# Small weight parts last in every split product, block 1 and the context in one pass, modulation steps in the middle MLP groups

## The chip, the core and the metric

The kernel runs on one core of one Trainium2 chip. The metric is the device time of one execution in microseconds (us). Three executions of the kernel before took 3923.38, 3931.42 and 3940.43 us, so the median is 3931.42 us. The profiled execution is another one, of 3930.93 us.

## What is computed

The reference is a backbone of two layers on 1024 latent tokens and 256 context tokens of width 1024. Each layer makes modulation vectors (six shift, scale and gate vectors of width 1024, for the latent tokens and for the context), a token mixer and an MLP with squared ReLU:

```python
for l in range(DEPTH):                                    # DEPTH = 2
    sh1, sc1, gt1, sh2, sc2, gt2 = adaln(c, w_ada[l], b_ada[l])        # silu(c) @ w + b, six parts
    csh1, ...                    = adaln(c_ctx, w_ada[l], b_ada[l])
    h_lat = rms_norm(x, g_attn_pre[l]) * (1 + sc1) + sh1               # h_ctx alike
    y_lat, y_ctx = hybrid_mixer(h_lat, h_ctx, ...)        # w_in; gated DeltaNet, RG-LRU, attention; w_out
    x = x + gt1 * rms_norm(y_lat, g_attn_post[l])
    h = rms_norm(x, g_mlp_pre[l]) * (1 + sc2) + sh2
    x = x + gt2 * rms_norm(square(relu(h @ w_mlp1[l])) @ w_mlp2[l], g_mlp_post[l])
    if l == 0:                                            # the context takes the same steps
        ctx = ...
```

In the last layer the context feeds the mixer, but its own output is not computed.

## The kernel before, in words

Activations are kept transposed, 128 channels on the partitions and tokens along the free axis. Tokens are cut in three blocks: "c" (256 context tokens), 0 and 1 (512 latent tokens each). The large products (w_in, w_out, both MLP matrices) are made with split operands: a weight tile `wr` of 128x1024 is loaded, ScalarE copies it to `wh` in a shorter format (the large part), and GpSimd subtracts to get `wl`, the small part (`weight`, L209; for the context alone VectorE makes every second `wl`). The activations are split in the same way: a tile `A` or `hid` holds both parts. `mm3` (L223) makes one output tile of 128 rows as 24 matmuls (12 in the second MLP matrix): for each of eight slices k of the contraction it multiplies large by large, large weight by small activation, small weight by large activation. Only the last of the three reads `wl`. The tags `wr`, `wh` and `wl` have two buffers each, so a weight's load starts when the split of the weight but one before it is done.

`layer` (L1151) first runs the mixer, then w_out (8 weights), then the MLP in eight groups of four weights up (w_mlp1) and four down (w_mlp2). w_out and the first two and last two MLP groups run as passes, one block at a time, each with its own loads of the weights; the four groups in the middle take all blocks with one load. The passes let the work between two products (`around`: the root mean square of the output, scale, residual, the next norm; two sums of squares by a product with `ones`, L186, and two broadcasts by transposes, L192) run behind the next pass. These four small products stand at fixed places in TensorE's stream, given as "behind the n-th output tile from here" (`put_behind`), and TensorE works in order, so it waits where they are not ready. In layer 0 the passes are 0, 1, "c"; in layer 1 they are 0, 1.

The modulation vectors are made by a list of background steps, `bg`. `tick(n)` (L321) takes up to n steps off the list. `weight` calls `tick(self.rate)`, `mla_attend` calls `tick(1)` for each chunk of keys, and `run` calls `tick(99)` once at the start. There are two kinds of step:

- `ada_pe` (L263): one step loads 128x1024 of w_ada and multiplies it on TensorE (two matmuls of 32x512). Layer 0's vectors 0 and 1 are made so at the start (16 loads, with eight buffers of their own); its vectors 2, 3 and 4 by 26 further steps (24 loads, 2 closing steps) that take the buffers of `wr`, one for each chunk of keys in the attention of layer 0.
- `ada_steps` (L294): one step loads 512x256 of w_ada into a `wr` buffer and accumulates it on VectorE in eight instructions; every second step closes with four one-column matmuls (L314). Vector 5 of a layer and vectors 0 to 4 of the next are made so: 48 steps in layer 0, 8 in layer 1. Before, the list is set after pass 0; one step goes with each weight of pass 1 (16 weights), the rest with the 32 weights of the middle groups.

All engines' orders are set when the program is built, by a scheduler that goes by priorities and its own estimates; on the chip each engine takes its instructions in that order, and SyncE's queue issues the loads and stores in its order.

Of the kernel before, what the change touches and what calls it, by code (L numbers as in the profile page):

```python
# [7 lines left out]
F32 = mybir.dt.float32  # L8
# [8 lines left out]
P = 128  # L17
D = 1024
KD = D // P
# [24 lines left out]
class Trunk:  # L44
    def __init__(self, tc, I, out, es):
        self.tc, self.nc, self.I, self.out = tc, tc.nc, I, out
        nc = self.nc
        self.cp = es.enter_context(tc.tile_pool(name="cp", bufs=1))
        self.open = {}
        self.wp = es.enter_context(tc.tile_pool(name="wp", bufs=1))  # L50
        self.tp = es.enter_context(tc.tile_pool(name="tp", bufs=1))
        self.dp = es.enter_context(tc.tile_pool(name="dp", bufs=1, space=DRAM))
        self.ps = es.enter_context(tc.tile_pool(name="ps", bufs=1, space=PSUM))
        self.n = self.ng = self.flip = self.ht = 0
        self.bg, self.rate, self.wpr = [], 0, 0
        self.held = []
        self.main = self.cur = ("s", (self.tp, 4), ["a", "st", "d"])
        self.cst = self.cp.tile([P, 5 * P], F32, name="cst")
        nc.sync.dma_start(self.cst, I["cst"])
        self.ident = self.cst[:, 0:128]  # L60
        self.mask = [self.cst[:, 128:256], self.cst[:, 256:384]]
        self.tri = [self.cst[:, 384:512], self.cst[:, 512:640]]
        self.ones = self.cp.tile([P, 128], F32, name="ones")
        nc.vector.memset(self.ones, 1.0)
        self.sil = self.cp.tile([P, KD, 32], F32, name="sil")
# [156 lines left out]

    def mm3(self, ps, w, acts, ks):  # L223

        nc = self.nc
        n, last = 0, 3 * len(ks) - 1
        for wk, a in zip(ks, acts):
            for wi, ai in ((0, 0), (0, 1), (1, 0)):
                mm = nc.tensor.matmul(ps, w[wi][:, wk, :], a[:, ai, :], start=n == 0, stop=n == last)  # L229
                n += 1  # L230
        for h in self.held:
            h[0] -= 1
            if h[0] == 0:
                for i in h[1]:
                    self.tc.add_manual_dep(i.ins, mm.ins.name, mybir.DependencyInfo(
                        mybir.DependencyClass.NoSync, mybir.DependencyReason.DATA), reason="behind")
        self.held = [h for h in self.held if h[0]]
# [82 lines left out]

    def tick(self, n):  # L321

        with self.later():
            for _ in range(n):
                if self.bg:
                    self.bg.pop(0)()


    def S(self, n):
        return self.xp.tile([P, 512], F32, tag="S", bufs=2, name=self.nm("S"))[:, :n]  # L330

    def prenorm(self, b, xs, s, L, which, behind=(0, 0)):

# [253 lines left out]
    def gdn_head(self, L, h, kss, qss, vd, last):  # L587

        nc = self.nc
        (kd, ssk, ktd), (qd, _, _) = kss, qss
        y, t, hv, rt, r2 = [self.small([P, NCH], "hk", 8) for _ in range(5)]
        self.rsqrt(y, ssk, t, hv)
        self.tt(rt, ssk, y, ALU.mult)
        self.tt(r2, y, y, ALU.mult)
        gv = dict(self.gv)
        hc8 = self.small([P, 3, NCH, 2], "hc8", 2)
        for i, k in enumerate(("nbeta", "beta", "bk")):
            gv[k] = hc8[:, i]  # L600
            self.tt(hc8[:, i], self.gv[k][:, :, h:8:4], r2.rearrange("p (c o) -> p c o", o=1).to_broadcast([P, NCH, 2]), ALU.mult)
        qbl = [0, 1] if last else BL
        kT, qT, vt = self.g5("kT"), self.g5("qT"), self.g5("vt").rearrange("p (c d) -> p c d", d=P)
        q0 = CTX if last else 0
        nc.sync.dma_start(kT, kd)
        nc.sync.dma_start(qT[:, q0:], qd[:, q0:])
        nc.sync.dma_start(vt, vd.rearrange("p (c d) -> p c d", d=P))
        self.tt(vt, vt, rt.rearrange("p (c o) -> p c o", o=1).to_broadcast([P, NCH, P]), ALU.mult, nc.gpsimd)
        N = [self.g5(f"N{d}").rearrange("p (c i) -> p c i", i=P) for d in range(2)]
        at = [self.g5(f"at{d}").rearrange("p (c i) -> p c i", i=P) for d in range(2)]  # L610
        Qg = [qT, self.g5("Qg1")]
        for b in BL:
            c0, w = GRP[b]
            qs = slice(c0 * P, (c0 + w) * P)
            x = None
            for d in range(2):
                hc = 4 * d + h
                bc = self.PT("ab"[d]).rearrange("p (c i) -> p c i", i=P)
                for i in range(w):
                    nc.tensor.transpose(bc[:, i, :], gv["G"][:, c0 + i, hc:hc + 1].to_broadcast([P, P]), self.ident)  # L620
                E = at[d][:, c0:c0 + w, :]
                self.tt(E, bc[:, 0:w, :], self.mask[d].rearrange("p (o i) -> p o i", o=1).to_broadcast([P, w, P]), ALU.add)
                for i in range(w):
                    self.act(E[:, i, :], E[:, i, :], AF.Exp, bias=gv["nG"][:, c0 + i, hc:hc + 1])
                if b in qbl:
                    if d == 0:
                        x = self.T()[:, :w * P]
                    self.act(Qg[1][:, qs] if d else x, bc[:, 0:w, :].rearrange("p c i -> p (c i)"), AF.Exp)
            pk = self.PT("c").rearrange("p (c i) -> p c i", i=P)
            for i in range(w):  # L630
                cs = slice((c0 + i) * P, (c0 + i + 1) * P)
                nc.tensor.matmul(pk[:, i, :], kT[:, cs], kT[:, cs], start=True, stop=True)
            for i in range(w):
                for d in range(2):
                    hc = 4 * d + h
                    c = c0 + i
                    self.stt(N[d][:, c, :], pk[:, i, :], gv["nbeta"][:, c, d:d + 1], at[d][:, c, :], ALU.mult, ALU.mult)
            if b in qbl:
                pq = self.PT("c").rearrange("p (c i) -> p c i", i=P)
                for i in range(w):  # L640
                    cs = slice((c0 + i) * P, (c0 + i + 1) * P)
                    nc.tensor.matmul(pq[:, i, :], kT[:, cs], qT[:, cs], start=True, stop=True)
                for d in range(2):
                    self.tt(at[d][:, c0:c0 + w, :], pq[:, 0:w, :], at[d][:, c0:c0 + w, :], ALU.mult)
                self.tt(Qg[1][:, qs], qT[:, qs], Qg[1][:, qs], ALU.mult, nc.gpsimd)
                self.tt(qT[:, qs], qT[:, qs], x, ALU.mult, nc.gpsimd)
        self.gdn_invert(N)
        return self.gdn_scan(h, gv, kT, ktd, vt, N, at, Qg, last)
# [493 lines left out]
    def layer(self, L, hs, xsrc, xdst_mid, xdst_end, nextL):  # L1142
# [20 lines left out]
                return self.prenorm(b, acc, s2, Ln, nwhich, behind[2:]) if Ln is not None else None  # L1163
        acc = newacc()
        h2, hn = {}, {}
        passes = [[b] for b in ([0, 1] if last else [0, 1, "c"])]
        xs = {b: self.fetch(xsrc, b, lp, "hidc" if b == "c" else "hid", 4 if b == "c" else 8) for b in obl}
        for b, in passes:
            n = BLK[b][1]
            ss = self.S(n)  # L1170
            for m in range(KD):
                w = self.weight(self.I["w_out"][l, m], weng([b], m))
                ps = self.M4(n)
                self.mm3(ps, w, ys[b], range(KD))
                self.act(acc[b][m], ps)
                self.sqsum(ss, acc[b][m], m == 0, nc.gpsimd)
            h2[b] = around(b, acc[b], ss, 0, xs[b], xdst_mid, L, 1,
                           {0: (1, 2, 6, 7), 1: (1, 2, 6, 7) if last else (2, 4, 9, 10), "c": (1, 2, 4, 5)}[b])

        acc = newacc()  # L1180
        ss = {}
# [2 lines left out]
        def up(bl, g):  # L1184
            hid = [{} for _ in range(4)]
            for f in range(4):
                w = self.weight(self.I["w_mlp1"][l, 4 * g + f], weng(bl, f))
                for b in bl:
# [1 line left out]
                    ps = self.M4(n)  # L1190
                    self.mm3(ps, w, h2[b], range(KD))

                    big = n == 512 or len(bl) == 1
                    a = lp.tile([P, 2, 512] if big else [P, 2, n], F32R, tag="hid" if big else "hidc",
                                bufs=8 if big else 4, name=self.nm("hid"))[:, :, :n]
                    r = self.T(0)[:, :n]
# [19 lines left out]
                        if g == NG - 1:  # L1216
                            self.sqsum(ss[b], acc[b][m], m == 0, nc.gpsimd)
        for bl in passes:
            self.rate = int(bl == [1])
            hid = [up(bl, g) for g in (0, 1)]  # L1220
            for g in (0, 1):
                down(bl, g, hid[g])
            if bl == [0]:
                self.bg = self.ada_steps(L, (5,)) + (self.ada_steps(nextL, (0, 1, 2, 3, 4)) if nextL else [])
        self.rate = 1
        for g in range(2, NG - 2):
            down(obl, g, up(obl, g))
        self.rate = 1
        for bl in passes:
            b = bl[0]  # L1230
            hid = [up(bl, g) for g in (NG - 2, NG - 1)]
            if b == 0:
# [12 lines left out]
    def new_layer(self, l):  # L1245
# [9 lines left out]
        self.ts(L.nw, L.cols("gnw"), 0.5, ALU.mult)  # L1255
        self.ts(L.hbi, L.cols("lbi"), 0.5, ALU.mult)

        x = self.small([P, 4], "sp4", 8)
        self.ts(x, L.cols("lam"), -1.0, ALU.mult)
        self.softplus(L.c4, x, lambda: self.small([P, 4], "sp4", 8))  # L1260
        self.ts(L.c2, L.c4, 2.0, ALU.mult)
        self.ts(L.c4, L.c4, -4.0, ALU.mult)
        return L
# [162 lines left out]
```

## Time and profile before

| | before |
|---|---|
| median of 3 runs | 3931.42 us |
| profiled execution | 3930.93 us |
| its span, first to last instruction | 3929.1 us |
| TensorE matmuls | 90% busy |
| TensorE weight loads | 70% |
| VectorE, ScalarE, GpSimd | 54%, 42%, 34% |
| granted TensorE clock, mean | 0.952 of full speed |
| DMA | 92 GB/s on average |

1.8 us of the profiled execution lie outside its span. TensorE's matmuls overlap in the records, so its busy share is not its rate: the distance from one matmul's start to the next one's is. In time order the span holds: the start (to 58 us), w_in and the DeltaNet heads of layer 0 (58 to 650), attention and RG-LRU (650 to 1006), w_out (1006 to 1144.6), the first MLP passes (1144.6 to 1446), the middle groups (1446 to 1913), the last passes (1913 to 2184.5); then layer 1: the mixer to 3053, w_out and the first passes to 3367, the rest to the end. PE is TensorE, PEld its weight loads, DVE VectorE, ACT ScalarE, POOL GpSimd, SP SyncE.

### The profile page before, as it was taken

Reading aid. Unit: us, or ns where it says so; the run is one execution under the profiler, and the core shown is the slowest. Engines: PE = TensorE matmul, PEld = TensorE weight load, DVE = VectorE, ACT = ScalarE, POOL = GpSimd, SP = SyncE. Lnnn points to the kernel's source line nnn. Section 1 sums busy time; section 2 is a strip of 40 time slices with the busy share of each in tenths; the row PEclk is TensorE's granted clock in tenths of the full one; section 3 lists DMA queues with packets and bytes.
Section 4 is the critical chain, followed back from the end, with each engine's and each line's share of the span. In section 5 each row is a group of like instructions: output and inputs, shape, how many; then the busy total and the mean of one; then the engine's idle time right before and its main releaser. Section 6 shows DMA issues by size and latency. Waiting matters only on the chain. (4 is left out here: it accounts for less than half of the span.)

```text
span 3929.1 us, 51637 instructions
## 1 busy us (share of the span) xinstructions
PE 3538.9 (90%) x19236; PEld 2757.1 (70%) x19236; DVE 2119.3 (54%) x4363; ACT 1657.7 (42%) x3501; POOL 1343.4 (34%) x931
## 2 busy tenths in 40 slices
PE   5999898888989889999998898997698999999998
PEld 3777786444767678888877777775455777888886
DVE  6667757667264544443356586677676263122124
ACT  3555454455354232222244355454555453222242
POOL 3211322344475231111266521112434673212254
PEclk8999999898989999999999999998799999999999
DMA  4221222322433442222344322223002434111143
GB/s 179 94 79 63 89 86 76 104 88 85 139 117 102 133 126 78 65 81 71 95 130 124 94 89 87 83 65 97 30 21 76 151 98 122 59 49 49 48 135 102
DMA packets 168380, 359.73 MB, mean 92 GB/s; under 512 B 15936, under 2 KB 74688, under 8 KB 168128
## 3 DMA queue, kind: packets, MB, share of 16 engines
q1 hardware_dynamic: 168128, 356.43, 28.8%
q8 instruction: 151, 2.47, 0.3%
q14 instruction: 101, 0.83, 0.1%
HBM read 290.57 MB, written 65.80 MB: 91 GB/s over the span
## 5 line engine op out<-in xcount | busy, mean ns | idle before, releaser
L138 POOL TENSOR_TENSOR wl<-wr,wh 128x1024 fp32r<-128x1024 f32 x292 | 713.4, 2443 | 1729.7 <-ACT wh L135 1707.7
L229 PE MATMUL mm<-A,wh 128*128 128x512 f32 (+1 forms) x3008 | 898.3, 380 | 21.3 <-DVE A L138 9.7
L135 ACT ACTIVATE wh<-wr 128x1024 fp32r<-128x1024 f32 x312 | 330.4, 1059 | 1085.4 <-PE mm L229 499.4
L229 PEld LDWEIGHTS mm<-A,wh 128*128 128x128 f32 x3008 | 551.2, 195 | 118.3 <-DVE A L138 12.0
L229 PE MATMUL mm<-A,wl 128*128 128x512 f32 (+1 forms) x1504 | 571.1, 380 | 14.6 <-POOL wl L138 13.2
L138 DVE TENSOR_TENSOR hid<-T,hid 128x512 fp32r<-128x512 f32 (+1 forms) x160 | 151.7, 950 | 432.5 <-ACT hid L135 432.5
L229 PE MATMUL mm<-hid,wh 128*128 128x512 f32 (+1 forms) x1280 | 376.8, 378 | 2.5 <-ACT wh L135 2.4
L229 PEld LDWEIGHTS mm<-A,wl 128*128 128x128 f32 x1504 | 292.4, 194 | 64.8 <-POOL wl L138 16.5
L229 PEld LDWEIGHTS mm<-hid,wh 128*128 128x128 f32 x1280 | 235.2, 191 | 50.0 <-ACT wh L135 4.1
L229 PE MATMUL mm<-hid,wl 128*128 128x512 f32 (+1 forms) x640 | 242.1, 379 | 16.3 <-DVE wl L138 11.2
L229 PE MATMUL pb<-A,wh 128*128 128x512 f32 (+1 forms) x800 | 239.1, 383 | 0.0
L229 PE MATMUL plr<-A,wh 128*128 128x512 f32 (+1 forms) x800 | 236.7, 380 | 1.4 <-ACT wh L135 1.4
L229 PE MATMUL pd<-A,wh 128*128 128x512 f32 (+1 forms) x704 | 235.6, 404 | 0.7 <-issue 0.7
L138 DVE TENSOR_TENSOR acc<-acc,mm 128x512 f32<-128x512 f32 (+1 forms) x140 | 88.6, 633 | 243.0 <-PE mm L229 234.6
L147 DVE SCALAR_TENSOR_TENSOR T<-raw,sm,T 128x512 f32<-128x512 f32 (+4 forms) x240 | 181.8, 760 | 43.5 <-ACT raw L135 21.6
L229 PE MATMUL plr<-hid,wh 128*128 128x512 f32 (+1 forms) x640 | 188.0, 378 | 6.1 <-DVE acc L138 4.0
L229 PE MATMUL pb<-hid,wh 128*128 128x512 f32 (+1 forms) x640 | 186.0, 375 | 0.0
L147 DVE SCALAR_TENSOR_TENSOR ada<-wa,sil,ada 128x256 f32<-128x256 f32 x392 | 172.3, 501 | 19.0 <-DMA wa<-in_w_ada_dram 18.7
L1025 PE MATMUL pd<-Pt,V 128*128 128x512 f32 (+1 forms) x336 | 165.9, 614 | 13.1 <-ACT Pt L135 9.7
L135 ACT ACTIVATE T<-T 128x512 f32<-128x512 f32 (+1 forms) x243 | 141.9, 584 | 84.9 <-DVE T L147 68.7
L138 POOL TENSOR_TENSOR S<-S,T 128x512 f32<-128x512 f32 (+1 forms) x126 | 162.7, 1292 | 30.1 <-ACT T L135 25.0
L229 PEld LDWEIGHTS plr<-A,wh 128*128 128x128 f32 x800 | 148.4, 193 | 31.4 <-ACT wh L135 2.1
(365 smaller groups left out, 7111.4 us busy)
## 6 DMA issues: line engine op xcount, KB each, us to landing
wr<-in_w_mlp_dram SPq DMA_DIRECT2D x224, 512.0 KB, 3.6
wa<-in_w_ada_dram SPq DMA_DIRECT2D x96, 512.0 KB, 3.7
wr<-in_w_in_dram SPq DMA_DIRECT2D x48, 512.0 KB, 3.7
wr<-in_w_out_dram SPq DMA_DIRECT2D x40, 512.0 KB, 3.7
A<-y SPq DMA_DIRECT2D x32, 256.0 KB, 3.1
xm<-acc SPq DMA_DIRECT2D x32, 256.0 KB, 4.2
x<-xm SPq DMA_DIRECT2D x16, 512.0 KB, 5.7
kT<-k SPq DMA_DIRECT2D x8, 640.0 KB, 4.1
```

The costliest lines, as they stand in the source:

```text
L135: return self.nc.scalar.activation(out, in_, f, **kw)
L138: return (eng or self.nc.vector).tensor_tensor(out, a, b, op=op)
L147: return self.nc.vector.scalar_tensor_tensor(out, a, s, b, op0=op0, op1=op1)
L229: mm = nc.tensor.matmul(ps, w[wi][:, wk, :], a[:, ai, :], start=n == 0, stop=n == last)
L1025: nc.tensor.matmul(po, V[:, c, :], p, start=ci == 0, stop=ci == len(chunks) - 1)
```

## The change

The core of the diff:

```diff
@@ mm3
-        for wk, a in zip(ks, acts):
-            for wi, ai in ((0, 0), (0, 1), (1, 0)):
+        for wi, ai in ((0, 0), (0, 1), (1, 0)):
+            for wk, a in zip(ks, acts):
@@ tick
+        self.due = self.due + n if self.bg else 0
         with self.later():
-            for _ in range(n):
-                if self.bg:
-                    self.bg.pop(0)()
+            while self.bg and self.due >= 1:
+                self.due -= 1
+                self.bg.pop(0)()
@@ S
-        return self.xp.tile([P, 512], F32, tag="S", bufs=2, name=self.nm("S"))[:, :n]
+        return self.xp.tile([P, n], F32, tag=f"S{n}", bufs=1 if n < 512 else 2, name=self.nm("S"))
@@ layer
-        passes = [[b] for b in ([0, 1] if last else [0, 1, "c"])]
+        passes = [[0], [1]] if last else [[0], [1, "c"]]
...
-            h2[b] = around(b, acc[b], ss, 0, xs[b], xdst_mid, L, 1,
-                           {0: (1, 2, 6, 7), 1: (1, 2, 6, 7) if last else (2, 4, 9, 10), "c": (1, 2, 4, 5)}[b])
+            for b in bl:
+                h2[b] = around(b, acc[b], ss[b], 0, xs[b], xdst_mid, L, 1,
+                               {0: (1, 2, 6, 7) if last else (1, 3, 8, 10), 1: (1, 2, 6, 7), "c": (2, 3, 8, 9)}[b])
...
         for bl in passes:
-            self.rate = int(bl == [1])
+            if len(bl) > 1:
+                for g in (0, 1):
+                    down(bl, g, up(bl, g))
+                continue
             hid = [up(bl, g) for g in (0, 1)]
             for g in (0, 1):
                 down(bl, g, hid[g])
-            if bl == [0]:
-                self.bg = self.ada_steps(L, (5,)) + (self.ada_steps(nextL, (0, 1, 2, 3, 4)) if nextL else [])
-        self.rate = 1
+        self.bg = self.ada_steps(L, (5,)) + (self.ada_steps(nextL, (0, 1, 2, 3, 4)) if nextL else [])
+        self.rate = 1.5 if nextL else 1
```

Five things change. In `mm3` all eight large-by-large products of an output tile come first, then the eight with the small activation part, then the eight that read `wl`; number and size are the same. In layer 0 block 1 and the context share w_out and the first two MLP groups, with one load of each weight for both: 24 weights fewer. The 48 and 8 `ada_steps` start only after the first passes, at 1.5 and 1 for each of the 32 weights of the middle groups. `tick` keeps a balance, `due`, so that it can take 1.5. And some tiles are smaller or have fewer buffers: the context's sums of squares have a tile of their own, the small tiles of the DeltaNet heads 6 buffers and not 8, those of the softplus at the start 4 and not 8. The last passes keep their order.

The balance is not cleared when a list ends with some of it left. `run` still calls `tick(99)` for the 17 steps of the start, then sets the list of 26 `ada_pe` steps of layer 0; `due` is 82 there. The first `weight` of w_in calls `tick(0)`, and all 26 go ahead of that weight.

SyncE's queue near the start, before: the last two of the 16 loads for vectors 0 and 1 (`wa`), then the weights of w_in (`wr`).

```order
L270 DMA wa_382<-in_w_ada_dram 128x1024
L270 DMA wa_386<-in_w_ada_dram 128x1024
L216 DMA wr_520<-in_w_in_dram 128x1024
L552 DMA ad_626<-in_alog_dt_dram 128x16
L216 DMA wr_688<-in_w_in_dram 128x1024
L216 DMA wr_834<-in_w_in_dram 128x1024
```

The same queue after the change, where the first weights of w_in stand now; the rows from `wa_521` to `wa_626` are the 24 loads for vectors 2, 3 and 4.

```order
L271 DMA wa_610<-in_w_ada_dram 128x1024
L271 DMA wa_614<-in_w_ada_dram 128x1024
L271 DMA wa_618<-in_w_ada_dram 128x1024
L271 DMA wa_622<-in_w_ada_dram 128x1024
L271 DMA wa_626<-in_w_ada_dram 128x1024
L216 DMA wr_640<-in_w_in_dram 128x1024
L216 DMA wr_808<-in_w_in_dram 128x1024
```

The 24 loads have moved from the attention of layer 0 to a place ahead of the first weight, and their products stand ahead of the first w_in product on TensorE.

TensorE in w_out of layer 0, before, at the end of block 1's first output tile (`plr`), with the sum of squares of block 0 (`pd`) and the next tile (`pb`), which has a new weight (numbers 9569, 9570).

```order
L229 MATMUL plr_9540<-A_8673,wh_9536 128x512 x2
L229 MATMUL plr_9540<-A_8673,wl_9537 128x512
L229 MATMUL plr_9540<-A_8674,wh_9536 128x512 x2
L229 MATMUL plr_9540<-A_8674,wl_9537 128x512
L186 MATMUL pd_9394<-ones,S_9115 128x1 x4
L229 MATMUL pb_9573<-A_8667,wh_9569 128x512 x2
L229 MATMUL pb_9573<-A_8667,wl_9570 128x512
```

The same place after the change.

```order
L230 MATMUL plr_9541<-A_8673,wh_9537 128x512
L230 MATMUL plr_9541<-A_8674,wh_9537 128x512
L230 MATMUL plr_9541<-A_8667,wl_9538 128x512
L230 MATMUL plr_9541<-A_8668,wl_9538 128x512
L230 MATMUL plr_9541<-A_8669,wl_9538 128x512
L230 MATMUL plr_9541<-A_8670,wl_9538 128x512
L230 MATMUL plr_9541<-A_8671,wl_9538 128x512
L230 MATMUL plr_9541<-A_8672,wl_9538 128x512
L230 MATMUL plr_9541<-A_8673,wl_9538 128x512
L230 MATMUL plr_9541<-A_8674,wl_9538 128x512
L186 MATMUL pd_9394<-ones,S_9115 128x1 x4
L230 MATMUL pb_9568<-A_8651,wh_9537 128x256
```

All products with `wl` have moved behind the 16 with `wh`, and the tile after block 1's is the context's (128x256), with the same weight, 9537.

SyncE's queue in pass 1 of the MLP, before, from its first `ada_steps` load on.

```order
L300 DMA wa_10953<-in_w_ada_dram 128x4x256
L216 DMA wr_10964<-in_w_mlp_dram 128x1024
L300 DMA wa_11001<-in_w_ada_dram 128x4x256
L216 DMA wr_11017<-in_w_mlp_dram 128x1024
L300 DMA wa_11054<-in_w_ada_dram 128x4x256
```

After the change the queue of the pass [1, "c"] holds no such load; the first stands at the first weight of the middle groups.

```order
L216 DMA wr_11883<-in_w_mlp_dram 128x1024
L301 DMA wa_11945<-in_w_ada_dram 128x4x256
L216 DMA wr_11956<-in_w_mlp_dram 128x1024
L301 DMA wa_12055<-in_w_ada_dram 128x4x256
L301 DMA wa_12071<-in_w_ada_dram 128x4x256
L216 DMA wr_12082<-in_w_mlp_dram 128x1024
```

One and two steps now go in turn with the weights of the middle groups.

More of the change, by code (lines that the diff above doesn't have):

```diff
@@ L54, in __init__ @@
         self.n = self.ng = self.flip = self.ht = 0
-        self.bg, self.rate, self.wpr = [], 0, 0
+        self.bg, self.rate, self.wpr, self.due = [], 0, 0, 0
         self.held = []
@@ L592, in gdn_head @@
         (kd, ssk, ktd), (qd, _, _) = kss, qss
-        y, t, hv, rt, r2 = [self.small([P, NCH], "hk", 8) for _ in range(5)]
+        y, t, hv, rt, r2 = [self.small([P, NCH], "hk", 6) for _ in range(5)]
         self.rsqrt(y, ssk, t, hv)
@@ L1165, in layer @@
         h2, hn = {}, {}
-        passes = [[b] for b in ([0, 1] if last else [0, 1, "c"])]
+        passes = [[0], [1]] if last else [[0], [1, "c"]]
         xs = {b: self.fetch(xsrc, b, lp, "hidc" if b == "c" else "hid", 4 if b == "c" else 8) for b in obl}
-        for b, in passes:
-            n = BLK[b][1]
-            ss = self.S(n)
+        ss = {}
+        for bl in passes:
+            for b in bl:
+                ss[b] = self.S(BLK[b][1])
             for m in range(KD):
[L1172 to L1176, printed above, removed]
-            h2[b] = around(b, acc[b], ss, 0, xs[b], xdst_mid, L, 1,
-                           {0: (1, 2, 6, 7), 1: (1, 2, 6, 7) if last else (2, 4, 9, 10), "c": (1, 2, 4, 5)}[b])
+                w = self.weight(self.I["w_out"][l, m])
+                for b in bl:
+                    ps = self.M4(BLK[b][1])
+                    self.mm3(ps, w, ys[b], range(KD))
+                    self.act(acc[b][m], ps)
+                    self.sqsum(ss[b], acc[b][m], m == 0, nc.gpsimd)
+            for b in bl:
+                h2[b] = around(b, acc[b], ss[b], 0, xs[b], xdst_mid, L, 1,
+                               {0: (1, 2, 6, 7) if last else (1, 3, 8, 10), 1: (1, 2, 6, 7), "c": (2, 3, 8, 9)}[b])
         acc = newacc()
@@ L1191, in up @@
                     self.mm3(ps, w, h2[b], range(KD))
-                    big = n == 512 or len(bl) == 1
+                    big = n == 512 or bl == ["c"]
                     a = lp.tile([P, 2, 512] if big else [P, 2, n], F32R, tag="hid" if big else "hidc",
@@ L1222, in layer @@
                 down(bl, g, hid[g])
-            if bl == [0]:
-                self.bg = self.ada_steps(L, (5,)) + (self.ada_steps(nextL, (0, 1, 2, 3, 4)) if nextL else [])
-        self.rate = 1
+        self.bg = self.ada_steps(L, (5,)) + (self.ada_steps(nextL, (0, 1, 2, 3, 4)) if nextL else [])
+        self.rate = 1.5 if nextL else 1
         for g in range(2, NG - 2):
             down(obl, g, up(obl, g))
-        self.rate = 1
-        for bl in passes:
+        for bl in [[b] for b in obl[-2:] + obl[:-2]]:
             b = bl[0]
@@ L1256, in new_layer @@
         self.ts(L.hbi, L.cols("lbi"), 0.5, ALU.mult)
-        x = self.small([P, 4], "sp4", 8)
+        x = self.small([P, 4], "sp4", 4)
         self.ts(x, L.cols("lam"), -1.0, ALU.mult)
-        self.softplus(L.c4, x, lambda: self.small([P, 4], "sp4", 8))
+        self.softplus(L.c4, x, lambda: self.small([P, 4], "sp4", 4))
         self.ts(L.c2, L.c4, 2.0, ALU.mult)
```

## The prediction

> **What bounds the kernel now.** I read the page first, then the matmuls of L229 (the split products) by stretch, then in each stretch who was waited for, and last the start in order of time.
>
> ```profile
> PE 3538.9 (90%) x19236; PEld 2757.1 (70%) x19236; DVE 2119.3 (54%) x4363; ACT 1657.7 (42%) x3501; POOL 1343.4 (34%) x931
> ```
>
> TensorE is the busiest engine, but its records overlap, so the 10% idle are not all that it loses. Its real rate is the distance between starts (start, length, then the instruction):
>
> ```profile
> 1644.81 0.63 PE L229 MATMUL plr<-hid,wh 128*128 128x512 f32 x2
> 1645.28 0.40 PE L229 MATMUL plr<-hid,wl 128*128 128x512 f32 x1
> 1645.51 0.40 PE L229 MATMUL pb<-hid,wh 128*128 128x256 f32 x2
> 1645.75 0.28 PE L229 MATMUL pb<-hid,wl 128*128 128x256 f32 x1
> 1645.87 0.40 PE L229 MATMUL pb<-hid,wh 128*128 128x256 f32 x2
> ```
>
> Three products of 512 columns take 0.70 us, three of 256 take 0.36. The split products by stretch (length; PE busy and count; weight loads; granted clock; DMA):
>
> ```profile
> 58.00:80.00 22.00, 15.21 (x50) 11.75 (x51) 0.65 0.10 30
> 1006.00:1108.60 102.60, 95.08 (x385) 73.78 (x386) 0.97 0.50 164
> 1108.60:1144.60 36.00, 26.69 (x193) 25.44 (x191) 0.91 0.46 137
> 1144.60:1259.60 115.00, 96.44 (x385) 75.54 (x386) 0.93 0.31 96
> 1259.60:1388.00 128.40, 103.63 (x386) 74.03 (x385) 0.95 0.40 127
> 1388.00:1446.00 58.00, 47.59 (x385) 45.67 (x383) 1.00 0.46 145
> 1446.00:1913.00 467.00, 465.44 (x2302) 385.49 (x2303) 1.00 0.24 74
> 1913.00:2184.50 271.50, 238.53 (x1154) 198.09 (x1154) 0.94 0.41 126
> 3053.00:3259.00 206.00, 188.82 (x768) 147.00 (x769) 0.97 0.41 127
> 3259.00:3367.00 108.00, 96.44 (x385) 74.20 (x384) 0.95 0.39 114
> 3367.00:3907.00 540.00, 539.16 (x2305) 433.13 (x2303) 1.00 0.24 72
> ```
>
> The last row is TensorE at its bound: 540/2305 = 0.234 us for each product of 512 at full clock. Half of it, 0.117, goes for 256. By these the others have a floor: 90.0 us for 384 products of 512, 22.5 for 192 of 256, 45.0 for 384 of 256. What is over the floor is what the change can reach: w_out 12.6 and 13.5, pass 0 25.0, pass 1 38.4, the context's pass 13.0, the last passes 271.5 - 225.0 = 46.5, in layer 1 206 - 180 = 26 and 108 - 90 = 18. Where there is excess the granted clock is below 1 (but for the context's pass), so a wait costs more than itself.
>
> The Trainium skill ("TensorE: Matmul & The Clock Gate", section on the HAM clock gate) says that about 3.4 us without work bring the clock to half until TensorE has been busy for a window again; these rows agree in that only stretches with waits are below 1.00.
>
> **The change part by part.**
>
> *Pass 1 and the context together.* In the stretch of pass 1 this is waited for longest, with the prices of a load, of both splits and of a step's instruction from the page:
>
> ```profile
> ACT wh L135 <- DMA wr<-in_w_mlp_dram: 68.9, 15, 8.5
> ...
> L138 POOL TENSOR_TENSOR wl<-wr,wh 128x1024 fp32r<-128x1024 f32 x292 | 713.4, 2443 | 1729.7 <-ACT wh L135 1707.7
> L135 ACT ACTIVATE wh<-wr 128x1024 fp32r<-128x1024 f32 x312 | 330.4, 1059 | 1085.4 <-PE mm L229 499.4
> L147 DVE SCALAR_TENSOR_TENSOR ada<-wa,sil,ada 128x256 f32<-128x256 f32 x392 | 172.3, 501 | 19.0 <-DMA wa<-in_w_ada_dram 18.7
> ...
> wr<-in_w_mlp_dram SPq DMA_DIRECT2D x224, 512.0 KB, 3.6
> ```
>
> A weight holds a `wr` buffer for 3.6 + 1.06 + 2.44 = 7.1 us, a step for 3.6 + 8 x 0.50 = 7.6. Two buffers give one pair in (7.1 + 7.6)/2 = 7.4 us at best, against 24 x 0.234 = 5.6 of products; measured are 128.4/16 = 8.0. Without steps a weight needs 7.1/2 = 3.6 us of the ring, and with the context its products last 8.4. So the joint pass is bound by products: 90.0 + 45.0 + 2 for first waits = 137 us in place of 128.4 + 58 = 186.4: **-49**. If the ring were late in spite of that cover, each weight would cost what it is late by; at most 16 x 1 us.
>
> *The steps in the middle.* With 1.5 steps a weight the ring needs (7.1 + 1.5 x 7.6)/2 = 9.3 us and VectorE 1.5 x 4.0 beside products of 450/32 = 14.1, so both stay hidden; what TensorE pays is the closing matmuls (L314 alone):
>
> ```profile
> 1446.00:1913.00 467.00, 17.73 (x128) 19.75 (x128) 1.00 0.24 74
> ```
>
> 17.73/16 = 1.1 us for each pair of steps, and 467 less its floor of 450 is about that sum. Eight pairs more are **+9** in layer 0; if the weight behind two steps in a row came 1 us late each time, 16 more. In layer 1 four pairs are **+5**.
>
> *Products with `wl` last.* An output tile can now run 16 products (3.7 us) before it needs `wl`, 1.9 us with the context alone, half of that in the second MLP matrix. The waits of TensorE in w_out of layer 0, its last passes, and w_out with pass 0 of layer 1, in this order:
>
> ```profile
> PE pb L229 <- DVE wl L138: 4.1, 1, 4.1
> PE pb L229 <- POOL wl L138: 3.7, 2, 3.0
> ...
> PE mm L229 <- DVE wl L138: 11.2, 1, 11.2
> PE mm L229 <- POOL wl L138: 5.3, 2, 3.8
> PE plr L229 <- POOL wl L138: 5.0, 3, 3.6
> ...
> PE plr L229 <- POOL wl L138: 6.4, 2, 3.4
> PE mm L229 <- DVE A L138: 3.3, 1, 3.3
> ```
>
> In w_out both stretches together are 26.1 over the floor; the context brings no weight of its own now, and I leave 6 for the small products in between: 112.5 + 6 in place of 138.6, **-20**. In the last passes the 5.3 goes, half of the 5.0 and 0.9 of the 11.2 (second matrix, context alone), and with the clock after them that is **-10**. In layer 1 the 9.7 go, with 5 of the 6 that a clock of 0.97 costs in 206, and pass 1 loses its steps (108 to 92): **-31**. The w_in stretches have few such waits: **-6**, from 0 to -12.
>
> A rule speaks against this order: each `wh` slice was used by two products in a row, and now no slice is. The Trainium skill (same title, the section on what each phase is for) has the weights loaded once and used for many products; by its formula a load of 128 columns takes 107 ns, an estimate by which a product of 256 columns still covers it and the sum stays. The profile counts as many loads as matmuls, and 1645.75 to 1645.87 is a change of slice at the same 0.12 us as the others: nothing is charged.
>
> *Pass 0.* Both `around` chains, block 1's and the context's, now run in its first half; before, half of block 1's ran behind the context's w_out. Its main wait was
>
> ```profile
> PE pd L186 <- POOL S L138: 11.4, 2, 7.5
> ...
> L138 POOL TENSOR_TENSOR S<-S,T 128x512 f32<-128x512 f32 (+1 forms) x126 | 162.7, 1292 | 30.1 <-ACT T L135 25.0
> ```
>
> The sums of squares go through POOL between the `wl`. Block 1's sum now has four output tiles (22 us) behind the broadcast; POOL needs 4 x 2.44 + 8 x 1.3 = 20 there. I take the same waits again, less `wl` and plus one weight that SyncE queues behind the context's stores: **+2**, from -10 to +25.
>
> *The 24 loads ahead of the first weight.* This is the term that the diff hides. The first products, and how such loads went in the attention:
>
> ```profile
> 43.03 0.55 SPq L216 DMA_DIRECT2D wr<-in_w_in_dram  x1
> ...
> 35.73 4.53 PE L272 MATMUL pb<-wa,sil 128*32 128x512 f32 x24
> 53.77 0.66 PE L282 MATMUL pb<-cst,T 128*128 128x128 f32 x4 [0.70 <-ACT T L135]
> 58.06 0.58 PE L229 MATMUL mm<-A,wh 128*128 128x256 f32 x1 [3.63 <-ACT A L135]
> ...
> 702.69 10.18 SPq L270 DMA_DIRECT2D wa<-in_w_ada_dram  x4
> 719.82 10.07 SPq L270 DMA_DIRECT2D wa<-in_w_ada_dram  x3
> ...
> DMA to landing us min/median/max: 3.6/4.2/14.2
> ```
>
> A load has four records; 24 of them in 4.53 us make 0.76 us a load at full clock, 1.5 at half. Two buffers of 4.2 + 0.76 to 1.5 give a load in 2.5 to 2.9 us; I take 2.8. The lower end is (3.6 + 0.76)/2 = 2.2; the upper is the attention's, where the four loads of 10.18 us are two pairs some 9 us apart, 4.4 a load, between other products. The first two go out near 43.03, where the first weight stood, and TensorE is free for them at 54.4. The first weight's own load follows 23 x 2.8 = 64 us later, and with 1.06 for `wh` the first product stands at 120 in place of 58: 62 us. Against that, the stretch 58 to 80 has 50 products with a floor of 9 at a clock of 0.65, because A was not ready; then it is, and 10 come back. **+52**, from +38 to +88. Nothing covers it: all of layer 0 waits for w_in.
>
> By the Trainium skill (the section on the clock gate) TensorE, never idle for 3.4 us at a stretch in this ring, would keep its full clock: with 2.5 us a load an estimate of 45 in place of 52.
>
> *The attention without them.* 24 x 0.76 = 18 us leave a stretch in which TensorE is this full:
>
> ```profile
> 740.00:790.00 50.00, 47.81 (x154) 21.75 (x153) 30.20 (x54) 20.74 (x44) 15.57 (x21) 1.00 0.26 79
> ```
>
> Other chains (softmax, RG-LRU) stand close behind: **-10**, from 0 to -20. Fewer buffers of the small tiles cost nothing: those of one head are long free at the next, and the softplus is off the way to the first norm.
>
> The sum is -49 - 20 - 10 - 31 - 6 - 10 + 2 + 9 + 5 + 52 = -58. The profiled execution took 3930.93, 0.5 under the median of the runs, so I predict **3873 us**.
>
> **The rivals.**
>
> - *The waits only move (13%).* `wh` or the load itself is late, so products with `wh` first find no weight. For it: TensorE waits for ACT too in pass 1. Against: outside that pass the rows name `wl`. Then w_out gains 8 and not 20, the last passes 3 and not 10, layer 1 20 and not 31, w_in none of its 6: 3873 + 36 = 3909.
> - *The two chains collide in pass 0 (12%).* The wait for S doubles, with the clock after it: +22, 3895. For it: 20 of 22 us of POOL. Against it: stores and sums of block 1 no longer stand between the context's short products.
> - *Slower: the ring of 24 is serial (5%).* One load at a time is 4.2 + 1.5 + 0.3 for the next issue = 6.0 us: the first product at 54.4 + 23 x 6.0 + 1 = 193, +125 in place of +52, and the attention gives nothing back: 3956. It decides from 4.9 us a load on, where the start costs the 100 that the rest brings. For it: SyncE's queue is in order, and each load waits for the products of the one but one before. Against it: the row at 702.69 has pairs in flight.
> - *The change of slice is not free (4%).* Of the context's products a third of 24 for each of 108 weights, 864, lose their repeated slice; at a weight load's record (433.13/2303 = 0.188) in place of 0.117 that is +61: 3934, no change. For it: the record; against it: the starts above.
> - *The attention gives all back and the ring runs at 2.5 (in the forecast's range)*: 3873 - 17 = 3856.
>
> **How the numbers follow.** The forecast has 62%, with 3845 to 3892 as its own range; 4% are left for what I don't see. 3845 to 3915 takes in the first two rivals, and leaves out the serial ring, the slice and the rest. Half a per cent, 20 us, is about what a measurement of this kernel can tell from none: faster is under 3912, slower over 3951. Faster: 62 + 12 + 7 (half of the first rival) + 2 = 83%. Same: 6 + 3 + 2 = 11%. Slower: 6%.
>
> **What would show it.** In the changed profile the first L230 product stands near 120 (106 to 157), with `wa` in a row before it; the joint pass takes about 137 us at a clock of 1.00; pass 0 still waits for S; waits for `wl` are gone but in the context's last pass; the middle of layer 0 takes about 476. I am wrong if the start costs over 110 us, if waits for `wh` take the place of those for `wl`, or if the joint pass is over 150.

## The result, and the profile after

The changed kernel takes 3880.4 us (median of four runs, 3869.3 to 3884.9) beside 3934.0 for the kernel before on the same chip: a ratio of 0.9862, with a 95% interval of 0.9831 to 0.9893. The profiled execution took 3882.8 us with a span of 3881.0. Predicted were 3873 us, 3845 to 3915.

TensorE has the same 19236 matmuls; VectorE, ScalarE and GpSimd lose the splits of 24 weights:

```profile
PE 3515.5 (91%) x19236; PEld 2749.3 (71%) x19236; DVE 2099.4 (54%) x4351; ACT 1646.9 (42%) x3477; POOL 1315.2 (34%) x919
```

The split products (now L230) by stretch, with the columns of the prediction's table: length; TensorE busy and count; weight loads; granted clock; DMA share and GB/s.

```profile
1041.30:1162.10 120.80, 115.44 (x577) 96.12 (x578) 0.99 0.43 140
1162.10:1269.90 107.80, 93.58 (x387) 72.51 (x386) 0.97 0.34 107
1269.90:1406.50 136.60, 135.28 (x769) 117.64 (x768) 1.00 0.22 67
1406.50:1878.30 471.80, 471.79 (x2306) 384.85 (x2305) 1.00 0.29 89
1878.30:2142.00 263.70, 234.06 (x1153) 195.18 (x1152) 0.95 0.41 130
3024.60:3128.40 103.80, 95.06 (x384) 74.73 (x384) 0.95 0.48 151
3128.40:3316.00 187.60, 182.53 (x770) 145.15 (x769) 0.99 0.34 102
3316.00:3859.00 543.00, 542.16 (x2303) 432.68 (x2302) 1.00 0.26 79
```

The rows are w_out of layer 0, pass 0, the joint pass, the middle, the last passes, then w_out, the first passes and the rest of layer 1. The joint pass has its 768 products at full clock in 136.6 us. Of these only pass 0, the last passes and w_out of layer 1 still have a clock well below 1.00.

SyncE's queue and TensorE at the start (start, length, the instruction, in brackets the wait before it):

```profile
54.82 61.19 SPq L271 DMA_DIRECT2D wa<-in_w_ada_dram  x22
118.65 10.51 SPq L216 DMA_DIRECT2D wr<-in_w_in_dram  x4
...
58.61 3.15 PE L273 MATMUL pc<-wa,sil 128*32 128x512 f32 x8 [3.72 <-DMA wa<-in_w_ada_dram]
...
123.51 3.78 PE L230 MATMUL mm<-A,wh 128*128 128x256 f32 x16 [0.63 <-ACT wh L135]
```

Twenty-two of the 24 loads go out within 61.19 us, 2.8 us each, and the first weight of w_in behind them; the first product stands at 123.5 us, where it stood at 58.06.

All kernels of this study have the same 11808 split products in the same stages, so a stage can be measured from its first product's start to the next stage's (the attention, which has none, from the start of w_in's last). In us, from one profiled execution each ("steps moved", "order alone": the kernel before with one edit; the four others in the middle: the changed kernel with one edit):

| stage | before | after | balance cleared | own passes | steps in joint pass | old order | order alone | steps moved alone |
|---|---|---|---|---|---|---|---|---|
| start | 58.1 | 123.5 | 56.9 | 122.1 | 124.5 | 123.9 | 56.9 | 57.8 |
| layer 0: w_in | 591.2 | 580.4 | 591.6 | 576.6 | 582.6 | 580.0 | 587.6 | 584.1 |
| attention | 356.8 | 337.4 | 354.5 | 337.6 | 337.0 | 337.5 | 353.9 | 356.3 |
| w_out | 138.9 | 120.7 | 119.3 | 136.1 | 120.7 | 124.8 | 133.6 | 136.9 |
| pass 0 | 114.6 | 107.8 | 108.2 | 113.9 | 108.2 | 114.3 | 116.2 | 115.4 |
| block 1 and context | 186.9 | 136.6 | 136.4 | 146.3 | 143.8 | 137.0 | 203.2 | 146.9 |
| middle | 467.1 | 471.8 | 471.8 | 472.7 | 464.1 | 471.1 | 465.7 | 472.6 |
| last passes | 271.1 | 263.7 | 265.9 | 263.9 | 264.7 | 268.1 | 265.0 | 270.0 |
| layer 1: w_in | 524.2 | 525.5 | 521.7 | 527.5 | 521.9 | 527.8 | 521.5 | 529.5 |
| attention | 344.5 | 357.1 | 357.2 | 353.6 | 356.0 | 346.7 | 356.3 | 343.7 |
| w_out, first passes | 313.6 | 291.4 | 289.4 | 291.4 | 289.6 | 294.3 | 308.9 | 296.0 |
| the rest | 562.1 | 564.9 | 565.3 | 564.9 | 565.3 | 564.4 | 561.3 | 564.8 |

What can't differ between two of these shows the noise: w_in of layer 0 in the kernels with the old order and a start as before reads 584 to 594, while the middle groups with the same steps agree within 2 us. A w_in is read to 5 us only.

### The profile page after: what moved, and what is told of

Same layout as the page of the kernel before. It is cut to its first block, busy times and chain, and to the rows that moved or that the text cites. A ratio compares the mean times of both kernels' runs of the same rounds, so it can differ in the third digit from the quotient of the medians.

```text
span 3881.0 us, 51471 instructions
## 1 busy us (share of the span) xinstructions
PE 3515.5 (91%) x19236; PEld 2749.3 (71%) x19236; DVE 2099.4 (54%) x4351; ACT 1646.9 (42%) x3477; POOL 1315.2 (34%) x919
## 5 line engine op out<-in xcount | busy, mean ns | idle before, releaser
L230 PE MATMUL mm<-A,wh 128*128 128x512 f32 (+1 forms) x3008 | 710.1, 380 | 2.9 <-POOL A L138 2.3
L230 PEld LDWEIGHTS mm<-A,wh 128*128 128x128 f32 x3008 | 524.8, 195 | 97.1 <-POOL A L138 2.7
L230 PE MATMUL mm<-A,wl 128*128 128x512 f32 (+1 forms) x1504 | 362.0, 374 | 1.4 <-DVE wl L138 1.4
L230 PE MATMUL mm<-hid,wh 128*128 128x512 f32 (+1 forms) x1280 | 302.7, 377 | 8.9 <-ACT T L135 6.8
L230 PEld LDWEIGHTS mm<-A,wl 128*128 128x128 f32 x1504 | 260.4, 191 | 48.4 <-DVE wl L138 1.6
L230 PEld LDWEIGHTS mm<-hid,wh 128*128 128x128 f32 x1280 | 227.7, 191 | 57.5 <-ACT T L135 7.2
L230 PE MATMUL pd<-A,wh 128*128 128x512 f32 (+1 forms) x704 | 193.7, 403 | 0.0
L230 PE MATMUL plr<-A,wh 128*128 128x512 f32 (+1 forms) x800 | 185.3, 383 | 0.0
L230 PE MATMUL pb<-A,wh 128*128 128x512 f32 (+1 forms) x800 | 173.0, 367 | 1.2 <-ACT wh L135 1.2
L230 PE MATMUL mm<-hid,wl 128*128 128x512 f32 (+1 forms) x640 | 166.4, 378 | 8.1 <-DVE wl L138 8.1
L230 PEld LDWEIGHTS plr<-A,wh 128*128 128x128 f32 x800 | 143.6, 188 | 31.3
L230 PE MATMUL plr<-hid,wh 128*128 128x512 f32 (+1 forms) x640 | 153.2, 381 | 13.0 <-DVE hid L138 9.9
L147 DVE SCALAR_TENSOR_TENSOR lr<-lr,lr 128x256 f32<-128x256 f32 x218 | 108.3, 507 | 91.4 <-POOL lr L138 85.8
```

Source lines behind the costliest of these rows:

```text
L147: return self.nc.vector.scalar_tensor_tensor(out, a, s, b, op0=op0, op1=op1)
```

## The experiments

**The balance cleared.** The 26 steps of vectors 2, 3 and 4 go back into the attention.

```diff
             self.tick(99)
+            self.due = 0
```

> The changed kernel with the balance set to zero behind the start's 17 steps, so that the 26 steps of vectors 2, 3 and 4 go one by one in the attention of layer 0 again. My theory (the 24 loads ahead of the first weight cost the start 55 us and give 19 back in the attention): first w_in product near 58 us and not 123.5, w_in done near 645 and not 704, attention of layer 0 near 357 and not 337, about 3845 us in all. Rival 1 (something else, the first norm, sets the start): first product later than 100 us, 3880. Rival 2 (TensorE does not bound the attention, its 19 us come from the order of the products): attention stays at 337, 3825.

Measured: 3840.2 us, ratio 0.9750 (0.9737 to 0.9763), 1.1% under the changed kernel's ratio. The start, then w_in and the attention (all engines' busy times: TensorE, weight loads, VectorE, ScalarE, GpSimd):

```profile
56.92 1.38 PE L230 MATMUL mm<-A,wh 128*128 128x256 f32 x3 [3.63 <-ACT A L135]
...
56.90:648.60 591.70, 535.34 (x4272) 444.89 (x4272) 412.97 (x1029) 304.57 (x865) 123.78 (x82) 0.96 0.24 80
648.60:1003.10 354.50, 307.13 (x1044) 165.80 (x1044) 226.74 (x439) 187.89 (x421) 144.03 (x182) 0.91 0.28 86
```

The same two stretches in the changed kernel:

```profile
123.50:703.90 580.40, 531.54 (x4272) 443.61 (x4272) 388.51 (x1000) 288.70 (x834) 109.52 (x69) 0.97 0.25 81
703.90:1041.30 337.40, 275.45 (x939) 166.88 (x939) 227.49 (x431) 184.89 (x419) 145.03 (x182) 0.87 0.18 55
```

The 24 loads cost the start 66.6 us; w_in gives 11.2 back, since all of A is ready by then (in the first 28.1 us from its first product on, TensorE waits 7.8 us for VectorE's part of A and starts 61 split products with the balance cleared, and here it has no such wait and starts 119), and the attention 17.1. Both rivals fall. In the attention TensorE is 31.7 us less busy (307.13 - 275.45) and the stage 17.1 shorter, close to the 18 that 24 x 0.76 make.

**Own passes for block 1 and the context**, with their own loads, the steps still in the middle only.

```diff
-        passes = [[0], [1]] if last else [[0], [1, "c"]]
+        passes = [[0], [1]] if last else [[0], [1], ["c"]]
...
-                w = self.weight(self.I["w_out"][l, m])
+                w = self.weight(self.I["w_out"][l, m], weng(bl, m))
```

> The changed kernel with block 1 and the context each in a pass of its own in layer 0, with loads of their own, but the modulation steps still only in the middle groups. My theory (in the 49 us of the joint pass both parts are needed little: without steps the ring is ahead of block 1's products; what sharing gives is the context's own loads): pass 1 about 95 us, the context's 50 to 58, together some 12 over the joint pass, w_out some 10 more: about 3903 us. Rival (sharing carries the 49): pass 1 stays near 128 and the whole goes to 3930.

Measured: 3909.2 us, ratio 0.9930 (0.9917 to 0.9942). Products of w_out, of block 1's pass and of the context's:

```profile
1036.20:1172.30 136.10, 121.00 (x576) 99.90 (x576) 0.94 0.50 157
1286.20:1376.00 89.80, 89.80 (x386) 72.33 (x385) 1.00 0.30 94
1376.00:1432.50 56.50, 49.14 (x386) 47.39 (x384) 0.97 0.46 142
```

Without steps block 1's pass needs no help from the context: 89.8 us is its floor. What sharing gives are the context's own loads: 15.4 us in w_out, 6.1 in pass 0, 9.7 here. With the passes the four small products of each `around` also go back to their old places in this run, so the 6.1 of pass 0 can be of either.

**The steps back in the joint pass**, one for each of its 16 weights.

```diff
             for g in (0, 1):
                 down(bl, g, hid[g])
-        self.bg = self.ada_steps(L, (5,)) + ...
-        self.rate = 1.5 if nextL else 1
+            if bl == [0]:
+                self.bg = self.ada_steps(L, (5,)) + ...
+                self.rate = int(not last)
+        self.rate = 1
```

> The changed kernel with one modulation step again for each of the 16 weights of the joint pass, the other 32 in the middle groups one by one. My theory (a weight's products last 8.4 us there, over the ring's 7.4 to 8.0 with steps): joint pass 137 + 8 pairs of steps at 1.1 = 146 us, middle groups of layer 0 463 and not 472, no change in all, 3880 us. Rival (a ring this near to the products is late at each weight, up to 1 us for 16): joint pass 160, 3896.

Measured: 3880.5 us, ratio 0.9852 (0.9838 to 0.9865), no difference from the changed kernel. The joint pass and the middle:

```profile
1273.20:1417.00 143.80, 142.71 (x770) 116.98 (x768) 1.00 0.39 118
1417.00:1881.10 464.10, 464.10 (x2307) 384.34 (x2306) 1.00 0.24 73
```

Eight pairs of steps cost 7.2 us in the joint pass and 7.7 in the middle, 0.9 to 1.0 a pair in either place, and the clock stays at 1.00: beside 8.4 us of products for each weight a ring of 8.0 is hidden.

**The steps moved alone**: the kernel before, with only the balance (cleared behind the start) and the steps in the middle groups.

```diff
-            self.rate = int(bl == [1])
...
-            if bl == [0]:
-                self.bg = self.ada_steps(L, (5,)) + ...
-        self.rate = 1
+        self.bg = self.ada_steps(L, (5,)) + ...
+        self.rate = 1.5 if nextL else 1
```

> The kernel before with the modulation steps in the middle groups alone (1.5 and 1 for each weight, the balance cleared): old order of the products, block 1 and the context in passes of their own. My theory (each of the two, the shared loads and the move of the steps, takes the steps' ring off the path by itself): block 1's pass and the context's together about 148 us and not 187, middle of layer 0 472 and not 467, first passes of layer 1 195 and not 214: 3938 - 39 + 5 - 19 + 4 = about 3889 us. Rival (the steps cost only beside the new order): 3930.

Measured: 3879.9 us, ratio 0.9845 (0.9829 to 0.9861): as much as the whole change. Block 1's pass and the context's, old order, no sharing:

```profile
1250.60:1340.40 89.80, 89.80 (x385) 72.33 (x384) 1.00 0.31 96
1340.40:1397.60 57.20, 47.46 (x386) 45.80 (x384) 1.00 0.45 143
```

128.4 us of block 1's pass become its floor of 89.8, with all its `wl` read in the old order. So the waits for `wl` in this pass came from the steps and not from the order of the products. That it was the steps' loads, in the two buffers that the weights use too, is argued from the waits there (`wh` for a weight's load); a step's other work went with them.

**The old order of the products** in the changed kernel.

```diff
-        for wi, ai in ((0, 0), (0, 1), (1, 0)):
-            for wk, a in zip(ks, acts):
+        for wk, a in zip(ks, acts):
+            for wi, ai in ((0, 0), (0, 1), (1, 0)):
```

> The changed kernel with the three products of each slice in a row again, all else kept. My theory (what ends last outside the joint pass is the small part of a weight): waits for wl come back in w_out (+10 us), pass 0 (+5), the last passes of layer 0 (+8), w_out and the first passes of layer 1 (+10) and w_in (+6); the joint pass stays at 137. If the order is also what made the mixer of layer 1 13 us longer, that goes: about 3906 us. If not, about 3919. Rival (the waits only moved from wl to wh): 3880 or less.

Measured: 3888.4 us, ratio 0.9874 (0.9861 to 0.9888); by their times the two kernels cannot be told apart. By the stages the new order gains 4.1 us in w_out, 6.5 in pass 0, 4.4 in the last passes, 2.9 in layer 1's w_out and first passes and nothing in w_in, and loses 10.4 in the attention of layer 1: 9 us of span in all. My theory, 26 us with the attention's part, was three times too large. Why, the last passes of layer 0 show. Waits of TensorE (us in total, times, longest) with the old order:

```profile
PE plr L230 <- POOL wl L138: 5.5, 3, 3.6
PE mm L230 <- DVE wl L138: 5.4, 2, 4.6
PE mm L230 <- POOL wl L138: 5.3, 2, 3.8
PE plr L230 <- DVE acc L138: 4.0, 1, 4.0
```

In the changed kernel, same passes:

```profile
PE plr L230 <- DVE hid L138: 9.9, 1, 9.9
PE mm L230 <- DVE wl L138: 9.5, 2, 8.1
PE plr L230 <- DVE acc L138: 3.1, 1, 3.1
```

GpSimd's 10.8 us of `wl` are gone, and TensorE waits 22.5 us for VectorE instead of 9.4.

**All small parts on GpSimd**, so that VectorE makes no `wl` in the context's last pass.

```diff
-            return nc.vector if bl == ["c"] and i % 2 else None
+            return None
```

> The changed kernel with every small weight part made on GpSimd, where in the context's last pass VectorE makes every second one. My theory (the 9.9 us wait for hid and the 9.5 for wl there are VectorE's queue, which the removed waits on GpSimd's wl gave way to): both shrink to 3 together and the last passes of layer 0 go from 264 to about 250 us, 3866 in all. Rival (GpSimd, with the sums of squares in its queue, is late in VectorE's place): last passes 264 or more, 3880 to 3890.

Measured: 3873.9 us, ratio 0.9839 (0.9818 to 0.9859), no difference; the last passes take 264.7. My theory falls: the waits change names.

```profile
PE mm L230 <- DVE acc L138: 7.9, 1, 7.9
PE plr L230 <- DVE hid L138: 3.9, 1, 3.9
PE pd L186 <- POOL S L138: 3.2, 1, 3.2
PE plr L230 <- DVE acc L138: 2.7, 1, 2.7
PE plr L230 <- ACT wh L135: 2.1, 1, 2.1
```

The accumulation, the hidden tile's split and the sum of squares come in turn late. Which of them would have to go for the pass to shorten stays open.

**The new order alone**, in the kernel before (the edit of the old order, reversed).

> The kernel before with the new order of the products alone. By the stages of the runs so far the order is worth little: w_out of layer 0 -4 us, pass 0 -6, last passes -4, first passes of layer 1 -7 but w_out there +4, and +10 in the attention of layer 1: about -7 us, 3932 beside 3939 on the same chip (ratio 0.998). Rival (my prediction's terms for this order, -6, -10, about -15 in layer 1 and -20 in w_out): 3890 to 3900.

Measured: 3920.3 us (ratio 0.9962, 0.9945 to 0.9980); its profiled execution, 3932.0, is the longest of its ten runs. The gain of some 15 us is above my 7 and far below the rival's 40. What I had not foreseen is block 1's pass, 143.3 us where it was 128.3, with a lower clock:

```profile
1248.20:1391.50 143.30, 114.58 (x386) 79.93 (x385) 0.88 0.35 114
...
PE mm L229 <- ACT wh L135: 19.3, 7, 4.7
PE plr L229 <- ACT wh L135: 5.7, 3, 2.6
```

The waits in the same pass of the kernel before, at a clock of 0.95:

```profile
PE mm L229 <- ACT wh L135: 6.4, 4, 2.7
PE mm L229 <- POOL wl L138: 6.2, 6, 1.8
PE plr L229 <- POOL wl L138: 4.0, 4, 1.3
```

Here the waits have moved from `wl` to `wh`, as the prediction's first rival said: the ring is late there, whichever part is read first. And they have come together: at most 2.7 us at a time before, up to 4.7 now. By the clock's records it fell to half eight times in this pass, and three times in the kernel before. The Trainium skill ("TensorE: Matmul & The Clock Gate", section on the HAM clock gate) puts the fall at about 3.4 us without work; the kernel before does not bear that out, since its clock fell with no wait over 2.7 us. All this is one execution, 11.6 us over its kernel's median; that the other nine have so long a pass is not shown.

**The old order in w_in only**, with the balance cleared.

```diff
-        for wi, ai in ((0, 0), (0, 1), (1, 0)):
-            for wk, a in zip(ks, acts):
+        three = ((0, 0), (0, 1), (1, 0))
+        ka = list(zip(ks, acts))
+        for (wi, ai), (wk, a) in [(t, q) for t in three for q in ka] if self.wpr else [(t, q) for q in ka for t in three]:
```

> The changed kernel with the balance cleared, and with the old order of the products in w_in alone; w_out and the MLP keep the new one. My theory (the new order in w_in brings nothing there and makes the scheduler put six VectorE instructions of the last DeltaNet head behind w_in, which is the attention's +10 in layer 1): attention of layer 1 near 346 and not 357, w_in of both layers unchanged, w_out of layer 1 100: 3840 - 11 = 3829 us. Rival (the attention's 10 us come from the smaller or fewer tile buffers): 3840.

Measured: 3836.6 us, ratio 0.9740 (0.9720 to 0.9760). The attention of layer 1 takes 346.1 us, as expected; but w_in there reads 526.1 and the joint pass 139.8, so the total cannot be told from that of the cleared balance alone. The first product of the last DeltaNet head's solve in the stretch, and its wait, here:

```profile
2662.47 0.26 PE L695 MATMUL pb<-X,N 32*32 32x32 f32 x2 [4.33 <-DVE X L689]
```

and in the changed kernel (L694 is the same line):

```profile
2704.54 0.26 PE L694 MATMUL pb<-X,N 32*32 32x32 f32 x2 [11.20 <-DVE X L688]
```

From the end of w_in (2638.1 and 2667.5) that is 24.4 and 37.0 us: the scheduler, which goes by its own estimates, gives VectorE the solve's column updates later when the products of w_in stand in the new order (23 pairs of them run behind the end of w_in where 18 did). The tile buffers have no part in it: the attention of layer 1 takes 353 to 357 us in every kernel with the new order in that w_in, the old buffers (order alone, 356.3) or the new, and 344 to 347 in every one with the old order.

**Eight buffers for the 24 loads**, still ahead of the first weight but for the last two, which the scheduler put behind it.

```diff
             self.tick(99)
+            self.due = 0
+            self.bg = self.ada_pe(Ls[0], (2, 3), xp, "wa", 8, "c") + self.ada_pe(Ls[0], (4,), xp, "wa", 8, "c")
+            self.tick(99)
...
-        self.bg = self.ada_pe(Ls[0], (2, 3), self.wp, "wr", 2, "c") + ...
```

> The changed kernel with the 24 loads of vectors 2, 3 and 4 still ahead of the first weight, but in the eight buffers of the first 16 loads and not in the two of wr. My theory (two buffers set 2.85 us a load, load and products in turn): with eight the loads are in flight together, at most 1.5 us each, and the first product stands at 123 - 24 x 1.3 = 92 us or earlier, with 5 to 10 of that given back in w_in: about 3855 us. Rival 1 (the transfers themselves, or TensorE at half clock, set the 2.85): first product stays at 120, 3880. Rival 2 (the first norm bounds from 58 on as in the kernel before, and the loads fit beside it): first product near 65, 3830.

Measured: 3837.8 us, ratio 0.9742 (0.9719 to 0.9765); the first product stands at 82.6 us. The ring, with two of its loads' products:

```profile
54.00:82.50 28.50, 22.02 (x90) 4.19 (x88) 22.88 (x35) 17.65 (x32) 17.43 (x12) 1.00 1.03 409
...
58.52 1.05 PE L273 MATMUL pc<-wa,sil 128*32 128x512 f32 x4 [0.23 <-DMA wa<-in_w_ada_dram]
59.80 1.05 PE L273 MATMUL pc<-wa,sil 128*32 128x512 f32 x4 [0.23 <-DMA wa<-in_w_ada_dram]
```

The changed kernel's ring of two:

```profile
54.00:122.00 68.00, 40.67 (x100) 4.59 (x92) 24.38 (x41) 17.62 (x33) 16.76 (x14) 0.60 0.57 178
98.50:122.00 23.50, 15.58 (x34) 1.54 (x32) 0.54 (x5) 0.45 (x1) 0.00 (x0) 0.50 0.56 177
```

1.28 us a load in place of 2.8, at 409 GB/s in place of 178: it was the two buffers, and rival 1 falls. With eight, the transfers are the bound (a DMA share of 1.03). My 3855 was 17 too high: the first product stands 25.7 us later than with the balance cleared, and w_in and the attention of layer 0 give 14 and 20 of it back.

**Eight buffers, and the old order in w_in of layer 1 alone**, for the best of all this.

> The changed kernel with the 24 loads in the eight buffers of the start, and with the old order of the products in w_in of layer 1 alone, for the best of what the runs so far showed. My theory: start and w_in of layer 0 as with eight buffers (first product at 83 us), attention of layer 1 near 346 and not 355, w_in of layer 1 some 4 longer: 3838 - 5 = 3832 us. Rival (what the attention gains w_in loses): 3838.

Measured: 3836.2 us, ratio 0.9735 (0.9718 to 0.9752). The attention of layer 1 takes 345.3 us and not 355.2, w_in before it 525.0 and not 519.7: what is left is below what these runs can tell. This, the old order in w_in, the eight buffers and the cleared balance all beat the changed kernel by 1.1 to 1.3% and cannot be told from one another; the cleared balance is the smallest edit.

## Why the prediction was right, and where its steps were not

The sign held, and so did the mechanisms of the two largest terms, the start and the joint pass; that of the order did not. The profile's difference, -48.1 us, is 10 from the sum of -58, and that is partly luck: by the table some terms were together 36 us too favourable and others 26 too unfavourable. By its steps:

- *The start*, +52: +54.6 to the end of w_in (649.3 to 703.9), with 2.8 us a load as taken, and 11 back for the 10. The serial ring did not come.
- *The joint pass*, 137: 136.6. But the working let both edits share the credit without saying that either would do. The steps' move alone takes the stage from 186.9 to 146.9, the sharing with steps in the pass to 143.8; the second of the two is worth 7 to 10 there.
- *The steps in the middle*, +9 and +5: +4.7 and +2.8. A pair costs 0.96, and the kernel before had 3 us more there than its pairs explain (467.1, beside 464.1 with as many steps).
- *The attention*, -10: mis-sized, -17 by the cleared balance (-19 in all). "Other chains stand close behind" was wrong; 17 of the 18 us of TensorE's work came off.
- *w_out of layer 0*, -20: -18.2, of which 12 to 15 are sharing and 1 to 5 the order; the working named the context's loads, but booked the whole under the order, beside the waits for `wl`.
- *Pass 0*, +2: -6.8. The waits for S did not return; what I left out is 6.5 us that the new order and the shared pass (with its new places) bring only together: with either alone the pass takes 113.9 to 116.2, as before. The rival of the two chains that collide did not come.

```profile
PE mm L230 <- ACT T L135: 6.8, 1, 6.8
PE pa L192 <- DVE n4s L147: 2.2, 1, 2.2
PE pd L186 <- POOL S L138: 0.5, 1, 0.5
```

- *Products with `wl` last*: the step that failed in size. It had -6 in w_in, -10 in the last passes and 15 of the -31 in layer 1, because the trace names `wl` as what ended last; and 3.3 of the 9.7 us that it let go in layer 1 are a wait for A, which this order cannot move. By the old order put back they are 0, -4.4 and -2.9. A wait's row gives what came last, not what comes next: behind `wl` stood VectorE's queue in the last passes, and `wh`, from the same ring, in block 1's pass. So the rival "the waits only move", given 13%, was half right: but for w_out the gains were near its sizes, while in the changed kernel the waits moved to VectorE and not to `wh` or the load.
- *Layer 1's w_out and first passes*, -31: -22.2. Their steps gave 17.6 (steps moved alone) for my 16; the rest is the line above.
- *Not in the sum*: the attention of layer 1, +12.6, 10.4 of it from the new order in w_in. That order of VectorE's work was fixed when the program was built, and the prediction left it out.

A ledger of the change by these runs, in spans: the steps' move -55 (steps moved alone), the 24 loads +43 (after less the balance cleared), the order -9 (after less the old order), which leaves -27 of the -48 to the shared pass, with the small products' new places and the smaller tiles, which no run separates. Each figure is from one execution of either kernel; by the ratios of the medians the first two are -61 and +44. By its stages the shared pass is worth 31 with the new order (own passes less after) and 23 with the old one (steps moved alone less old order). One part alone gives what all five give together, because an uncleared counter takes what the sharing and the order add.

## What to carry to other kernels

A wait in the profile names what came last; before a gain is booked in full, find what would have come next, and whether a common cause (here two ring buffers with a step's load between the weights) feeds both. When a list of background work is paced by a counter, look at what the counter holds when the next list begins. After a change of order in one stage, compare the order of the other stages too, since a scheduler that goes by estimates moves their work with it.

## What the runs showed of the hardware

- In the ring of two buffers the clock went up and down, and from 98.03 us to 128.75 it stayed at 0.50. Four stretches of it in a row (length; TensorE busy and count; granted clock; DMA), and the waits from 98.5 to 122:

```profile
70.73:74.14 3.41, 2.98 (x8) 0.50 0.48 143
74.14:77.56 3.42, 1.05 (x4) 1.00 0.63 205
77.56:94.62 17.06, 11.53 (x24) 0.50 0.58 174
94.62:98.03 3.41, 1.29 (x6) 1.00 0.65 209
...
PE pc L273 <- DMA wa<-in_w_ada_dram: 6.7, 7, 1.7
```

The clock's records have stretches of 3.41 us and its multiples, and what goes with a change is how much of such a window TensorE was busy. In the trace of the changed kernel each of the 48 falls comes behind a window with at most 2.3 us of work, no window with under 1.5 us kept the full clock, and each rise within the span comes behind one with at least 2.7 us; in all twelve traces no window under 1.4 us kept it, and no rise came with under 2.7. Between the two marks, and now and then above them, it went either way. That fits both rings. A load in 2.8 us brings 1.05 us of products at full clock (1.3 in 3.41, and the clock falls) and 1.92 at half (2.3 in 3.41, mostly too little to rise); with eight buffers, 1.05 us in every 1.28 are 2.8 in 3.41, and it stayed at 1.00. The rule that the prediction cited by the Trainium skill's section on the HAM clock gate (a fall after about 3.4 us without work) does not give this: the falls at 70.73, 77.56 and 98.03 came with waits of 2.5 us at most. The same title's section on a second failure mode tells of brief, frequent idling that makes the clock go up and down, for another queue; the rows above show the same with DMA waits.
- Eight loads of 512 KB in flight reached 409 GB/s on one core. The Trainium skill ("DMA: Bandwidth & Descriptors", section on bandwidth) has 425 GB/s for one transfer of 16 MB, issued from GpSimd; the trace comes near it with many loads of 512 KB, issued from SyncE.
